# Two decoder blocks on one core: the first modulation, tokens and weight slabs in four groups, and element-wise work moved to GpSimd

## The chip, the core and the metric

The kernel runs on one core of one Trainium2 chip. The metric is the device time of one execution in microseconds (us), the median of the runs shown. TensorE (PE) multiplies matrices, VectorE (DVE) and ScalarE (ACT) do element-wise work, GpSimd (POOL) has been left almost without work so far, and SyncE (SP) issues nearly all DMAs.

## The reference, cut to what matters

512 tokens of width 1024 go through two blocks in float32. The change touches only the beginning of the first:

```
c_act = silu(c)
mod   = c_act @ ada_w + ada_b            # 6 parts of 1024: sh1, sc1, gt1, sh2, sc2, gt2
h     = rms_norm(x, norm_mix_g) * (1 + sc1) + sh1
p     = h @ w_in                          # 896 columns of RWKV, then 512, 768, 256 and 4096 others
y_a   = rwkv7_mixer(p[...])               # y_b: spatial gating, y_c: short convolution, y_d: S5
merged = sum of sigmoid(gate) * y over the four branches
```

The S5 mixer needs tables that depend on its parameters alone: powers of a complex decay (`pw`), times an input matrix (`bb`) or an output matrix (`c4`), for 8 steps each. They are `Q` and `W2`, each a real and an imaginary tile of 128x1024.

## The kernel before, in words

Tokens are kept transposed: 8 tiles of 128 features x 512 tokens. A float32 product is made in three matmuls: each factor is split into an upper half `hi` (ACT, rounded to a type that TensorE takes in one pass) and a lower half `lo` (DVE, the difference), and `mm3` multiplies hi·hi, lo·hi and hi·lo. A weight slab (`wload`) is 128x1024: a DMA into `raw`, `whi` on ACT, `wlo` on DVE. A projection (`proj`) is one slab times the 8 token tiles: 24 matmuls of 128x512.

`_start` opens the program. It broadcasts c over all partitions, makes silu (ACT and DVE), and computes 8 columns of the modulation, each as a DVE dot product of a 128x1024 tile of `ada_w` with `c_row` (`_dot`, shown as CUSTOM_DVE_ANT_0). This is done in two groups of 4 columns; behind each stand 4 token tiles, scaled by `g1` = (1 + sc1) · norm gain and split, and a slab. The RMS norm is not waited for: the seven slabs of RWKV are multiplied with the tokens before their norm, and the rows are scaled afterwards by `rs` (which `means`, `factors` and `spread` make from the sums of squares). `_start_shift` then makes 8 more columns of the modulation and the finished `h`, which every later projection uses. The convolution branch (`cg`, `cy`), the spatial gating (`svp`, `sgz`, `sgm`) and the merges follow.

`_s5_setup` makes the powers with some 120 DVE instructions of a few columns each, `_s5_tables` makes Q and W2 (12 tensor-tensor instructions of 128x1024 by `_cmul`, one negation) and the phases `ph`. TensorE transposes Q (`s5q`) and multiplies it (`s5k`) just before it multiplies `sgm`, which needs `sgz`.

Each engine runs its own queue in order. A scheduler lays the queues out when the program is built; `issue_after(i)` keeps a block's instructions behind instruction i on i's engine. Line numbers are those of the kernel before; in the changed one `_start`'s and later lines stand some 30 to 40 further down.

Of the kernel before, what the change touches and what calls it, by code (L numbers as in the profile page):

```python
# [25 lines left out]
KD = 8  # L26
# [66 lines left out]
class _Core:  # L93
# [230 lines left out]
def _dot(K, raw, src, row, out, scale=1.0, after=None):  # L324

    K.nc.sync.dma_start(raw, src)
    with K.tc.issue_after(after) if after is not None else nullcontext():
        K.nc.vector.tensor_tensor_reduce(raw, raw, row, scale, 0.0, OP.mult, OP.add, out)  # L328


def _ada(K, cols, tag=None, after=None):

    for j in cols:
        if tag is None:
            raw = K.wpool.tile([128, K.WMAX], F32, name="raw", tag="raw", bufs=4)[:, 0:1024]
# [28 lines left out]

def _start(K):

    nc, V = K.nc, K.nc.vector
    K.modv = K.const.tile([128, 48], F32, name="modv")
    K.c_row = K.g("c_row", "cr", shape=(128, D))
    c = K.g("c", "e4", shape=(128, D))  # L370
    nc.sync.dma_start(c, K.dram["c"].partition_broadcast(128))
    nc.scalar.activation(K.c_row, c, AF.Tanh, scale=0.5)
    V.scalar_tensor_tensor(K.c_row, K.c_row, 1.0, c, OP.add, OP.mult)
    g1 = K.const.tile([128, 8], F32, name="g1")
    x, K.h, K.ahead = [], [], []
    for q in range(2):
        ks = slice(4 * q, 4 * q + 4)
        for _ in _ada(K, range(8 + 4 * q, 12 + 4 * q), "e4"):
            pass
        V.scalar_tensor_tensor(g1[:, ks], K.modv[:, 8 + 4 * q:12 + 4 * q], 1.0, K.vec("norm_mix_g", 4 * q, 4),  # L380
                               OP.add, OP.mult)
        if q == 0:
            K.ahead.append(K.wload(K.dram["w_in"][A_ORDER[0]], 8, 128))
        for k in range(4 * q, 4 * q + 4):
            x.append(K.g(f"x{k}", "xr"))
            nc.sync.dma_start(x[k], K.dram["x"][k])
            K.h.append(K.split(x[k], "h", g1[:, k:k + 1]))
        if q == 0:
            K.ahead.append(K.wload(K.dram["w_in"][A_ORDER[1]], 8, 128))
    K.tables()  # L390
    K.split_1 = K.last
    with K.tc.issue_after(K.last):
        v = K.means(K.squares(x, tag="yd"))
    y = K.factors(v, "x")
    K.factored = nc.cur_bb.bb.instructions[-1]
    return x, g1, K.spread(y)


def _start_shift(K, x, g1, rs):
# [363 lines left out]
    return st  # L763


def _rwkv(K, x, g1, rs):

    nc, d = K.nc, K.dram
    tiles = []
    for i, j in enumerate(A_ORDER):  # L770
        ps = K.proj(d["w_in"][j], K.h, w=K.ahead.pop(0) if K.ahead else None)
        p = K.g("rp", "rk")
        nc.scalar.copy(p, ps)
        tiles.append(p)
        if i == SHIFT_AT:
            h = _start_shift(K, x, g1, rs)
    K.h = h
    return tiles


def _rwkv_shift(K, ps, rs):

    nc, d, V = K.nc, K.dram, K.nc.vector
    row = [K.g("sh_row", "yd") for _ in range(2)]
    _row(K, K.modv, row)
    part = K.const.tile([128, 2, 7], F32, name="rk_sp")
    for i, j in enumerate(A_ORDER):
        for q in range(2):
            raw = K.g("w_t", "yd")
            _dot(K, raw, d["w_in_t"][j][:, q * 512:(q + 1) * 512], row[q], part[:, q, j:j + 1],  # L790
                 after=K.sg_normed)
    mu, mu1 = K.vec("rwkv_mu", 0, 7), K.const.tile([128, 7], F32, name="mu1")
    V.tensor_scalar(mu1, mu, -1.0, 1.0, OP.mult, OP.add)
    sv = K.const.tile([128, 2, 7], F32, name="rk_sv")
    V.tensor_tensor(sv[:, 0], part[:, 0], part[:, 1], OP.add)
    V.scalar_tensor_tensor(sv[:, 1], sv[:, 0], -1.0, mu, OP.mult, OP.mult)
    tiles = []
    for p, j in zip(ps, A_ORDER):
# [12 lines left out]
    return la, [tiles[1:4], tiles[4:7]]
# [191 lines left out]
def _s5_tables(K, sp, z):  # L1003
# [8 lines left out]
    w = [128, 8, 8, 16]  # L1012
    pk = lambda z, o: z[:, :, o:o + 8].unsqueeze(3).to_broadcast(w)
    mk = lambda z: z.unsqueeze(2).to_broadcast(w)
    _cmul(V, v4(Q[0]), v4(Q[1]), pk(pr, 0), pk(pi, 0), mk(bb[:, 0]), mk(bb[:, 1]), v4(tq))
    _cmul(V, v4(W2[0]), v4(W2[1]), pk(pr, 1), pk(pi, 1), mk(c4[:, 0]), mk(c4[:, 1]), v4(tq))
    V.tensor_scalar(W2[1], W2[1], -1.0, None, OP.mult)

    cb = K.g("s5_cb", "e", shape=(128, 2, 8, 32))
    nc.gpsimd.memset(cb, 0.0)  # L1020
# [144 lines left out]
def _first_block(K):  # L1165
    nc, d = K.nc, K.dram
    with ExitStack() as mix:
        tags = lambda **n: mix.enter_context(K.tags(**n))
        tags(h=16, y=8, yd=4, rk=8, cr=1)
        tags(space=PSUM, mm=3, sm=5)  # L1170
        tags(side="right", tm=2)
        ada = _ada(K, range(16, 48))
        with K.tags(e=9, e4=8):
            with K.tc.tile_pool(name="s5", bufs=1) as sp:
                x, g1, rs = _start(K)
                tiles = _rwkv(K, x, g1, rs)
# [36 lines left out]
def _feed_forward(K):
# [457 lines left out]
```

## Time and profile before

| what | value |
|---|---|
| median of 3 runs | 2148.33 us (2146.29 to 2150.67) |
| the profiled execution's own time | 2149.2 us |
| its span, first to last instruction | 2147.4 us |
| PE busy | 2094.6 us, 98% of the span |
| DVE busy | 1416.1 us, 66% |
| ACT busy | 934.1 us, 43% |
| POOL busy | 23.5 us, 1% |
| mean granted TensorE clock | 0.992 |

The profiled execution took 1.8 us more than its span, and was 0.9 us above the median. Busy shares are means over stages with different limits; what the change is worth is read in the first 150 us.

### The profile page before, as it was taken

What the parts mean: (1) busy time and instruction counts of PE and PEld (TensorE: products, weight loads), DVE (VectorE), ACT (ScalarE), POOL (GpSimd) and SP (SyncE); (2) the same over time, 40 slices, a digit from 0 to 9 for tenths busy, and PEclk for the clock granted to TensorE, in tenths of its full rate; (3) what the DMA queues carried; (4) which work ended last, traced back from release to release, by engine and by line L of the source; (5) the groups of instructions that cost most, each with busy time, mean ns of one, the idle gap of its engine ahead of it and who ended that gap; (6) DMA issues with size and microseconds to landing.
All of it is one profiled execution on the core that took longest, in us unless ns stands there. A gap on an engine that the chain in (4) does not pass through costs nothing.

```text
span 2147.4 us, 29518 instructions
## 1 busy us (share of the span) xinstructions
PE 2094.6 (98%) x11502; PEld 1692.7 (79%) x11502; DVE 1416.1 (66%) x2655; ACT 934.1 (43%) x1549; POOL 23.5 (1%) x44
## 2 busy tenths in 40 slices
PE   6999999999999999999999999999999999999998
PEld 4877787888888888897778888888887778788887
DVE  7997884755734344558876756747568867575775
ACT  3334432333523232446764423324469944243433
POOL 0010000000000000000000000000000000000000
PEclk9999999999999999999999999999999999999999
DMA  8355441123322232232212222232321122323222
GB/s 329 106 182 180 159 148 50 60 84 133 108 98 89 98 98 89 99 119 89 80 50 98 98 93 94 89 98 81 128 79 40 60 79 86 101 83 105 97 81 67
DMA packets 68091, 220.47 MB, mean 103 GB/s; under 512 B 8068, under 2 KB 11060, under 8 KB 67952
## 3 DMA queue, kind: packets, MB, share of 16 engines
q1 hardware_dynamic: 64704, 210.19, 29.6%
q0 software_dynamic: 2096, 6.30, 1.0%
q8 instruction: 91, 1.49, 0.3%
q10 hardware_dynamic: 1152, 2.10, 0.3%
q14 instruction: 48, 0.39, 0.1%
HBM read 215.25 MB, written 3.30 MB: 102 GB/s over the span
## 4 chain that ended last, share of the span: by engine, by line
PE 85%; DVE 6%; ACT 4%; DMA 2%; issue 1%; DVEq 0%; ACTq 0%; SPq 0%
PE mm L174 62%; PE gp L174 7%; PE vt L174 3%; PE yp L174 2%; DMA raw<-ada_w 2%; PE pT L1336 1%; DVE wlo L153 1%; PE po L1349 1%; PE fin L174 1%; PE s L1316 1%; PE s L1317 1%; ACT whi L152 1%; DVE raw L328 1%; ACT p L1324 1%; PE pmt L643 1%
## 5 line engine op out<-in xcount | busy, mean ns | idle before, releaser
L174 PE MATMUL mm<-hi,whi 128*128 128x512 f32 x2088 | 829.7, 398 | 19.1 <-ACT hi L161 17.8
L174 PE MATMUL mm<-hi,wlo 128*128 128x512 f32 x2088 | 830.5, 398 | 1.1 <-DVE wlo L153 1.1
L174 PE MATMUL mm<-lo,whi 128*128 128x512 f32 x2088 | 829.2, 397 | 1.1 <-DVE lo L165 0.5
L152 ACT ACTIVATE whi<-raw 128x1024 fp32r<-128x1024 f32 (+3 forms) x341 | 350.3, 1030 | 754.9 <-PE mm L174 600.9
L153 DVE TENSOR_TENSOR wlo<-raw,whi 128x1024 fp32r<-128x1024 f32 (+3 forms) x341 | 403.5, 1186 | 180.2 <-ACT whi L152 170.7
L174 PEld LDWEIGHTS mm<-hi,whi 128*128 128x128 f32 x2088 | 395.7, 190 | 110.3 <-ACT hi L161 20.8
L174 PEld LDWEIGHTS mm<-lo,whi 128*128 128x128 f32 x2088 | 394.9, 189 | 91.1 <-DVE lo L165 2.7
L174 PEld LDWEIGHTS mm<-hi,wlo 128*128 128x128 f32 x2088 | 394.7, 189 | 89.9 <-DVE wlo L153 2.0
L1521 DVE TENSOR_TENSOR u<-mm,spr 128x512 f32<-128x512 f32 x88 | 60.6, 688 | 82.5 <-PE mm L174 82.2
L174 PE MATMUL gp<-hi,wlo 128*128 128x512 f32 x256 | 102.7, 401 | 3.3 <-DVE wlo L153 3.3
L174 PE MATMUL gp<-hi,whi 128*128 128x512 f32 x256 | 104.1, 407 | 0.9 <-ACT whi L152 0.9
L174 PE MATMUL gp<-lo,whi 128*128 128x512 f32 x256 | 102.9, 402 | 0.0
L1541 DVE TENSOR_TENSOR x<-x,mm 128x512 f32<-128x512 f32 x48 | 33.0, 687 | 96.1 <-PE mm L174 96.1
L1240 DVE SCALAR_TENSOR_TENSOR x<-mm,modv,x 128x512 f32<-128x512 f32 x32 | 24.0, 751 | 91.0 <-PE mm L174 91.0
L1522 ACT ACTIVATE cv<-u,vecs 128x512 f32<-128x512 f32 x88 | 71.3, 810 | 3.4 <-DVE u L1521 3.2
L1524 DVE SCALAR_TENSOR_TENSOR cv<-u,vecs,cv 128x510 f32<-128x510 f32 x88 | 66.0, 750 | 3.1
L1523 DVE SCALAR_TENSOR_TENSOR cv<-u,vecs,cv 128x511 f32<-128x511 f32 x88 | 65.6, 746 | 2.3 <-ACT cv L1522 2.1
L1532 ACT ACTIVATE cth<-cv 128x512 f32<-128x512 f32 x44 | 27.8, 632 | 86.2 <-DVE cv L1524 86.2
L174 PEld LDWEIGHTS gp<-hi,wlo 128*128 128x128 f32 x256 | 48.4, 189 | 15.6 <-DVE wlo L153 5.1
L1324 ACT ACTIVATE p<-p,at_m 128x128 f32<-128x128 f32 (+1 forms) x96 | 53.4, 557 | 14.7 <-DVE at_m L1323 13.7
L174 PEld LDWEIGHTS gp<-hi,whi 128*128 128x128 f32 x256 | 48.6, 190 | 13.4 <-ACT whi L152 1.8
L174 PEld LDWEIGHTS gp<-lo,whi 128*128 128x128 f32 x256 | 48.6, 190 | 10.6 <-issue 0.4
(532 smaller groups left out, 2612.1 us busy)
## 6 DMA issues: line engine op xcount, KB each, us to landing
raw<-w_up SPq DMA_DIRECT2D x88, 512.0 KB, 3.3
raw<-ffn_w SPq DMA_DIRECT2D x64, 512.0 KB, 3.3
raw<-w_in SPq DMA_DIRECT2D x49, 512.0 KB, 3.4
raw<-ada_w SPq DMA_DIRECT2D x32, 512.0 KB, 3.9
raw<-w_down SPq DMA_DIRECT2D x32, 384.0 KB, 3.1
ada_w<-ada_w SPq DMA_DIRECT2D x16, 512.0 KB, 8.7
raw<-w_out SPq DMA_DIRECT2D x16, 512.0 KB, 3.4
raw<-w_down SPq DMA_DIRECT2D x16, 512.0 KB, 3.3
```

What stands on the lines that cost most here:

```text
L152: nc.scalar.activation(hi[:, :n], raw[:, :n], AF.Copy)
L153: nc.vector.tensor_tensor(lo[:, :n], raw[:, :n], hi[:, :n].bitcast(F32), OP.subtract)
L174: self.nc.tensor.matmul(out, lhsT=a, rhs=b, start=first and n == 0, stop=last and n == total - 1)
L328: K.nc.vector.tensor_tensor_reduce(raw, raw, row, scale, 0.0, OP.mult, OP.add, out)
L1240: V.scalar_tensor_tensor(K.xr[m], ps, K.modv[:, 40 + m:41 + m], K.xr[m], OP.mult, OP.add)
L1324: A.activation(p[:, 0:n], p[:, 0:n], AF.Exp, bias=nm, scale=-1.0, accum_out=l)
L1521: V.tensor_tensor(u, ps, rs, OP.mult)
L1522: A.activation(c, u, AF.Identity, bias=K.vec("conv_b_2", l * 44 + j), scale=tap(2))
L1523: V.scalar_tensor_tensor(c[:, 1:], u[:, 0:S - 1], tap(1), c[:, 1:], OP.mult, OP.add)
L1524: V.scalar_tensor_tensor(c[:, 2:], u[:, 0:S - 2], tap(0), c[:, 2:], OP.mult, OP.add)
L1532: A.activation(th, gt, AF.Tanh, scale=0.5)
L1541: V.tensor_tensor(K.xr[m], K.xr[m], ps, OP.add)
```

## The change

`_start` takes modulation, tokens and slabs in four groups of two instead of two groups of four; c comes in two halves. The first three slabs are loaded there (two before), and their products are issued group by group, two token tiles at a time. Their lower halves, and the additions of the sums of squares, are GpSimd instructions. The squares are queued behind the last `hi` on ACT. Two small DVE instructions that need `vecs` (`mu1`, `gg`) and the S5 setup are queued further back. In `_s5_tables` the 12 products for Q and W2 and the negation are GpSimd instructions.

```diff
 def _start(K):
-    nc.sync.dma_start(c, K.dram["c"].partition_broadcast(128))
-    nc.scalar.activation(K.c_row, c, AF.Tanh, scale=0.5)
-    V.scalar_tensor_tensor(K.c_row, K.c_row, 1.0, c, OP.add, OP.mult)
+    for q in range(2):
+        o = slice(q * 512, (q + 1) * 512)
+        nc.sync.dma_start(c[:, o], K.dram["c"][o].partition_broadcast(128))
+        nc.scalar.activation(K.c_row[:, o], c[:, o], AF.Tanh, scale=0.5)
+        V.scalar_tensor_tensor(K.c_row[:, o], K.c_row[:, o], 1.0, c[:, o], OP.add, OP.mult)
...
-    for q in range(2):
-        ks = slice(4 * q, 4 * q + 4)
-        for _ in _ada(K, range(8 + 4 * q, 12 + 4 * q), "e4"):
-            pass
...
+    def slab():
...
+        nc.sync.dma_start(raw, K.dram["w_in"][A_ORDER[len(w)]])
+        nc.scalar.activation(hi, raw, AF.Copy)
+        G.tensor_tensor(lo, raw, hi.bitcast(F32), OP.subtract)
...
+    def products(i, k0, k1):
+        for k in range(k0, k1):
+            K.mm3(ps[i], [(w[i][0][:, k], w[i][1][:, k])], K.h[k:k + 1], first=k == 0, last=k == KD - 1)
...
+    def squares(k0):
+        for k in (k0, k0 + 1):
+            sq = acc if k == 0 else K.g("rms_q", "yd")
+            with K.tc.issue_after(K.hi_last):
+                nc.scalar.activation(sq, x[k], AF.Square)
+            if k:
+                G.tensor_tensor(acc, acc, sq, OP.add)
...
+    for q in range(4):
+        ks = slice(2 * q, 2 * q + 2)
+        for j in range(8 + 2 * q, 10 + 2 * q):
+            _dot(K, K.g("ada_w", "e4", shape=(128, 1024)), K.dram["ada_w"][j], K.c_row, K.modv[:, j:j + 1], 0.5)
...
         if q == 0:
-            K.ahead.append(K.wload(K.dram["w_in"][A_ORDER[0]], 8, 128))
-        for k in range(4 * q, 4 * q + 4):
+            slab()
+        for k in range(2 * q, 2 * q + 2):
             x.append(K.g(f"x{k}", "xr"))
             nc.sync.dma_start(x[k], K.dram["x"][k])
             K.h.append(K.split(x[k], "h", g1[:, k:k + 1]))
-        if q == 0:
-            K.ahead.append(K.wload(K.dram["w_in"][A_ORDER[1]], 8, 128))
+        if q:
+            squares(2 * q - 2)
+        if q < 2:
+            slab()
+        for i in range(min(q + 2, 3) if q else 2):
+            products(i, done[i], 2 * q + 2)
+            done[i] = 2 * q + 2
...
 def _s5_tables(K, sp, z):
...
-    _cmul(V, v4(Q[0]), v4(Q[1]), pk(pr, 0), pk(pi, 0), mk(bb[:, 0]), mk(bb[:, 1]), v4(tq))
-    _cmul(V, v4(W2[0]), v4(W2[1]), pk(pr, 1), pk(pi, 1), mk(c4[:, 0]), mk(c4[:, 1]), v4(tq))
-    V.tensor_scalar(W2[1], W2[1], -1.0, None, OP.mult)
+    G = nc.gpsimd
+    _cmul(G, v4(Q[0]), v4(Q[1]), pk(pr, 0), pk(pi, 0), mk(bb[:, 0]), mk(bb[:, 1]), v4(tq))
+    _cmul(G, v4(W2[0]), v4(W2[1]), pk(pr, 1), pk(pi, 1), mk(c4[:, 0]), mk(c4[:, 1]), v4(tq))
+    G.tensor_scalar(W2[1], W2[1], -1.0, None, OP.mult)
...
 def _first_block(K):
-                with K.tc.issue_after(K.split_1):
+                with K.tc.issue_after(last):
                     z = _s5_setup(K, sp)
```

On GpSimd's queue, before, a memset of the S5 branch was followed directly by another, and then by the store of `s5_kt`:

```order
L1020 MEMSET s_cb 128x512
L1045 MEMSET s_ti_1745 128x1024
L1041 DMA s_scr<-s_kt 128x256
```

Now, between the same two memsets, stand the lower halves, the sums of squares and the S5 tables (the negation of `s_W_1684` and four more products follow, not shown):

```order
L1060 MEMSET s_cb 128x512
L389 ISA
L389 TENSOR_TENSOR wlo<-raw,whi 128x1024 x2
L405 TENSOR_TENSOR rms_a<-rms_a,rms_q 128x512
L389 TENSOR_TENSOR wlo<-raw,whi 128x1024
L405 TENSOR_TENSOR rms_a<-rms_a,rms_q 128x512 x6
L981 TENSOR_TENSOR s_Q_1681<-s_pw,s_bb 128x1024
L982 TENSOR_TENSOR s_tq<-s_pw,s_bb 128x1024
L984 TENSOR_TENSOR s_Q_1682<-s_pw,s_bb 128x1024
L983 TENSOR_TENSOR s_Q_1681<-s_Q_1681,s_tq 128x1024
L981 TENSOR_TENSOR s_W_1683<-s_pw,s_bc 128x1024
L985 TENSOR_TENSOR s_tq<-s_pw,s_bb 128x1024
```

DVE, in the convolution branch (`cg`, `cy`), had the tables between that branch's instructions and the lower halves of its slabs:

```order
L947 TENSOR_TENSOR s_bb<-s_bb,s_tb 128x128
L870 SCALAR_TENSOR_TENSOR cy<-cg,vecs,cy 128x510
L942 TENSOR_TENSOR s_Q_1674<-s_pw,s_bb 128x1024
L943 TENSOR_TENSOR s_tq<-s_pw,s_bb 128x1024
L863 TENSOR_TENSOR cg<-mm,cg 128x512
L153 TENSOR_TENSOR wlo<-raw,whi 128x1024
L870 SCALAR_TENSOR_TENSOR cy<-cg,vecs,cy 128x511
L944 TENSOR_TENSOR s_Q_1674<-s_Q_1674,s_tq 128x1024
```

In the changed program, behind the last instructions for `bb`, DVE goes on with the convolution branch and the decay of the phases (`s_mag`, `s_sn`), and the products of the tables are gone from its queue:

```order
L983 TENSOR_TENSOR s_bb<-s_bb,s_tb 128x128
L153 TENSOR_TENSOR wlo<-raw,whi 128x1024
L985 TENSOR_TENSOR s_tb<-s_bc,s_qi 128x128
L911 TENSOR_TENSOR cy<-mm,cy 128x512
L986 TENSOR_TENSOR s_bb<-s_bb,s_tb 128x128
L153 TENSOR_TENSOR wlo<-raw,whi 128x1024
L164 TENSOR_TENSOR lo<-cy,hi 128x512
L1096 TENSOR_TENSOR s_mag<-s_mag 128x8
```

Behind the last lower half of the tokens, DVE had the additions of the squares, with the S5 setup between them:

```order
L264 TENSOR_TENSOR rms_a<-rms_a,rms_q 128x512
L961 TENSOR_SCALAR s_lre<-s_par 128x8
L962 COPY s_x<-s_par 128x8
L264 TENSOR_TENSOR rms_a<-rms_a,rms_q 128x512
L202 TENSOR_SCALAR s_x<-s_x 128x8
```

There it now has the two instructions that need `vecs`, and then the norm (`rms_v` waits for TensorE's `rms_p`, which waits for GpSimd's last addition):

```order
L832 TENSOR_SCALAR mu_1636<-vecs 128x7
L1287 TENSOR_TENSOR gg<-vecs 128x8
L276 TENSOR_SCALAR rms_v<-rms_p 128x4
L191 TENSOR_SCALAR rms_y<-rms_v 128x4
L192 TENSOR_SCALAR rms_y<-rms_y 128x4
L153 TENSOR_TENSOR wlo<-raw,whi 128x1024
```

## Rows read from the trace of the kernel before

**Rows 1.** Busy time by engine, from the page: us (share of span) xinstructions.
```profile
PE 2094.6 (98%) x11502; PEld 1692.7 (79%) x11502; DVE 1416.1 (66%) x2655; ACT 934.1 (43%) x1549; POOL 23.5 (1%) x44
```

**Rows 2.** Stages: stretch, length, busy us (xinstructions) by engine, granted clock, DMA, GB/s.
```profile
14.95:29.24 14.29, 11.95 (x34) 8.29 (x35) 12.29 (x21) 7.38 (x12) 0.00 (x0) 1.00 0.99 365
...
44.30:73.00 28.70, 28.70 (x130) 23.47 (x129) 26.84 (x53) 13.10 (x20) 0.96 (x1) 1.00 0.35 118
73.00:100.00 27.00, 27.00 (x119) 21.88 (x118) 26.72 (x99) 8.04 (x10) 0.00 (x0) 1.00 0.29 93
100.00:129.20 29.20, 25.74 (x188) 23.95 (x186) 28.09 (x68) 13.63 (x27) 0.55 (x1) 0.93 0.53 182
140.10:250.00 109.90, 106.33 (x573) 86.81 (x572) 85.19 (x166) 45.07 (x82) 2.51 (x3) 0.98 0.55 177
```

**Rows 3.** Timeline of the start, DVE and PE: start us, length us, engine, line, instruction.
```profile
14.95 0.80 PE L174 MATMUL mm<-hi,whi 128*128 128x512 f32 x1 [14.95 <-ACT hi L161]
...
26.50 2.74 DVE L165 SCALAR_TENSOR_TENSOR lo<-x,g,hi 128x512 fp32r<-128x512 f32 x4 [0.79 <-ACT hi L161]
```

**Rows 4.** Timeline of DVE, around the finished h and the gating.
```profile
37.10 0.16 DVE L275 TENSOR_SCALAR rms_v<-rms_p 128x4 f32<-128x4 f32 x1 [0.52 <-PE rms_p L272]
...
70.92 0.74 DVE L410 SCALAR_TENSOR_TENSOR lo<-x,modv,hi 128x512 fp32r<-128x512 f32 x1
...
128.74 0.74 DVE L917 TENSOR_TENSOR sgz<-sgz,sg_ln 128x256 f32<-128x256 f32 x2
```

**Rows 5.** Timeline of PE: pace of the third slab and the last matmul ahead of `h`.
```profile
37.50 0.63 PE L174 MATMUL mm<-hi,whi 128*128 128x512 f32 x1
37.93 0.63 PE L174 MATMUL mm<-lo,whi 128*128 128x512 f32 x1
...
43.68 0.39 PE L174 MATMUL mm<-lo,whi 128*128 128x512 f32 x1
43.91 0.40 PE L174 MATMUL mm<-hi,wlo 128*128 128x512 f32 x1
```

**Rows 6.** Timeline of PE at the end of the gating's projections.
```profile
117.78 1.95 PE L350 MATMUL row_p<-k_ident,modv 128*128 128x128 f32 x16
119.57 2.18 PE L1031 MATMUL s5q<-k_ident,s_Q 128*128 128x128 f32 x16
...
129.21 1.12 PE L928 MATMUL sgm<-sg_wsT,sgz 128*64 128x128 f32 x8 [3.43 <-DVE sgz L917]
```

**Rows 7.** ACT's first copy of the gating's products, timeline.
```profile
106.57 0.37 ACT L248 COPY gl_x<-svp 128x256 f32<-128x256 f32 x1 [4.04 <-PE svp L174]
```

**Rows 8.** Two of the table products on DVE, timeline.
```profile
88.97 1.22 DVE L942 TENSOR_TENSOR s_Q<-s_pw,s_bb 128x1024 f32<-128x1024 f32 x1
90.10 1.22 DVE L943 TENSOR_TENSOR s_tq<-s_pw,s_bb 128x1024 f32<-128x1024 f32 x1
```

**Rows 9.** POOL's memsets, groups of instructions.
```profile
L1045 POOL MEMSET s_ti<- 128x1024 f32 x2 | 1.9, 964 | 50.6 <-DVE modv L328 50.6
...
L1020 POOL MEMSET s_cb<- 128x512 f32 x1 | 0.6, 563 | 0.0
```

**Rows 10.** POOL's and DVE's timelines around one memset, then around the other.
```profile
132.04 0.97 POOL L1045 MEMSET s_ti<- 128x1024 f32 x1
...
131.71 1.33 DVE L1059 TENSOR_SCALAR s_sn<-s_t 128x8 f32<-128x8 f32 x1
131.78 1.25 DVE L195 SCALAR_TENSOR_TENSOR bn_y<-bn_t,bn_y 128x2 f32<-128x2 f32 x1
131.86 1.19 DVE L1060 TENSOR_SCALAR s_xr<-s_s 128x8 f32<-128x8 f32 x1
...
54.14 0.96 POOL L1045 MEMSET s_ti<- 128x1024 f32 x1 [50.61 <-DVE modv L328]
...
54.69 4.06 DVE L407 SCALAR_TENSOR_TENSOR x<-x,g,spr 128x512 f32<-128x512 f32 x6
```

**Rows 11.** DVE's negation of a table, timeline.
```profile
129.48 0.68 DVE L1017 TENSOR_SCALAR s_W<-s_W 128x1024 f32<-128x1024 f32 x1
```

More of the change, by code (lines that the diff above doesn't have):

```diff
@@ L161, in split @@
         nc.scalar.activation(hi[:, :n], src, AF.Copy, scale=scale)
+        self.hi_last = nc.cur_bb.bb.instructions[-1]
         if isinstance(scale, float) and scale == 1.0:
@@ L365, in _start @@
 def _start(K):
-    nc, V = K.nc, K.nc.vector
+    nc, V, G = K.nc, K.nc.vector, K.nc.gpsimd
     K.modv = K.const.tile([128, 48], F32, name="modv")
@@ L370, in _start @@
     c = K.g("c", "e4", shape=(128, D))
-    nc.sync.dma_start(c, K.dram["c"].partition_broadcast(128))
-    nc.scalar.activation(K.c_row, c, AF.Tanh, scale=0.5)
-    V.scalar_tensor_tensor(K.c_row, K.c_row, 1.0, c, OP.add, OP.mult)
-    g1 = K.const.tile([128, 8], F32, name="g1")
-    x, K.h, K.ahead = [], [], []
-    for q in range(2):
-        ks = slice(4 * q, 4 * q + 4)
-        for _ in _ada(K, range(8 + 4 * q, 12 + 4 * q), "e4"):
-            pass
-        V.scalar_tensor_tensor(g1[:, ks], K.modv[:, 8 + 4 * q:12 + 4 * q], 1.0, K.vec("norm_mix_g", 4 * q, 4),
-                               OP.add, OP.mult)
+    for q in range(2):
[3 more added lines that the diff above has]
+        V.scalar_tensor_tensor(K.c_row[:, o], K.c_row[:, o], 1.0, c[:, o], OP.add, OP.mult)
@@ new lines, in _start @@
+    K.acted = nc.cur_bb.bb.instructions[-1]
+    g1 = K.const.tile([128, 8], F32, name="g1")
+    x, K.h, w, ps = [], [], [], []
+    def slab():
+        raw = K.wpool.tile([128, K.WMAX], F32, name="raw", tag="raw", bufs=4)[:, 0:1024]
+        hi = K.wpool.tile([128, K.WMAX], F32R, name="whi", tag="whi", bufs=3)[:, 0:1024]
+        lo = K.wpool.tile([128, K.WMAX], F32R, name="wlo", tag="wlo", bufs=3)[:, 0:1024]
+        nc.sync.dma_start(raw, K.dram["w_in"][A_ORDER[len(w)]])
+        nc.scalar.activation(hi, raw, AF.Copy)
+        G.tensor_tensor(lo, raw, hi.bitcast(F32), OP.subtract)
+        w.append([t.rearrange("p (k c) -> p k c", k=8) for t in (hi, lo)])
+        ps.append(K.mm())
@@ new lines, in products @@
+    def products(i, k0, k1):
+        for k in range(k0, k1):
+            K.mm3(ps[i], [(w[i][0][:, k], w[i][1][:, k])], K.h[k:k + 1], first=k == 0, last=k == KD - 1)
+    acc = K.g("rms_a", "yd")
+    def squares(k0):
[5 more added lines that the diff above has]
+                G.tensor_tensor(acc, acc, sq, OP.add)
+    done = [0, 0, 0]
@@ L382, in _start @@
+    for q in range(4):
+        ks = slice(2 * q, 2 * q + 2)
+        for j in range(8 + 2 * q, 10 + 2 * q):
+            _dot(K, K.g("ada_w", "e4", shape=(128, 1024)), K.dram["ada_w"][j], K.c_row, K.modv[:, j:j + 1], 0.5)
+        m = K.modv[:, 8 + 2 * q:10 + 2 * q]
+        V.tensor_tensor(m, m, K.vec("ada_b", 8 + 2 * q, 2), OP.add)
+        V.scalar_tensor_tensor(g1[:, ks], m, 1.0, K.vec("norm_mix_g", 2 * q, 2), OP.add, OP.mult)
         if q == 0:
-            K.ahead.append(K.wload(K.dram["w_in"][A_ORDER[0]], 8, 128))
@@ L387, in _start @@
             K.h.append(K.split(x[k], "h", g1[:, k:k + 1]))
-        if q == 0:
-            K.ahead.append(K.wload(K.dram["w_in"][A_ORDER[1]], 8, 128))
+        if q:
[5 more added lines that the diff above has]
+            done[i] = 2 * q + 2
     K.tables()
     K.split_1 = K.last
-    with K.tc.issue_after(K.last):
-        v = K.means(K.squares(x, tag="yd"))
+    squares(6)
+    v = K.means(acc)
     y = K.factors(v, "x")
     K.factored = nc.cur_bb.bb.instructions[-1]
-    return x, g1, K.spread(y)
+    return x, g1, K.spread(y), ps
 def _start_shift(K, x, g1, rs):
@@ L763, in _wkv_consts, with _rwkv @@
     return st
-def _rwkv(K, x, g1, rs):
+def _rwkv(K, x, g1, rs, ahead):
     nc, d = K.nc, K.dram
@@ L770, in _rwkv @@
     for i, j in enumerate(A_ORDER):
-        ps = K.proj(d["w_in"][j], K.h, w=K.ahead.pop(0) if K.ahead else None)
+        ps = ahead[i] if i < len(ahead) else K.proj(d["w_in"][j], K.h)
         p = K.g("rp", "rk")
@@ L792, in _rwkv_shift @@
     mu, mu1 = K.vec("rwkv_mu", 0, 7), K.const.tile([128, 7], F32, name="mu1")
-    V.tensor_scalar(mu1, mu, -1.0, 1.0, OP.mult, OP.add)
+    with K.tc.issue_after(K.split_1):
+        V.tensor_scalar(mu1, mu, -1.0, 1.0, OP.mult, OP.add)
     sv = K.const.tile([128, 2, 7], F32, name="rk_sv")
@@ L1174, in _first_block @@
             with K.tc.tile_pool(name="s5", bufs=1) as sp:
-                x, g1, rs = _start(K)
-                tiles = _rwkv(K, x, g1, rs)
+                x, g1, rs, ahead = _start(K)
+                tiles = _rwkv(K, x, g1, rs, ahead)
                 last = K.last
-                with K.tc.issue_after(K.split_1):
+                with K.tc.issue_after(last):
                     z = _s5_setup(K, sp)
@@ L1245, in _feed_forward @@
     gg = K.const.tile([128, 8], F32, name="gg")
-    V.tensor_tensor(gg, K.vec("final_g", 0, 8), K.vec("norm_mix_2", 0, 8), OP.mult)
+    with K.tc.issue_after(K.split_1):
+        V.tensor_tensor(gg, K.vec("final_g", 0, 8), K.vec("norm_mix_2", 0, 8), OP.mult)
     x = [K.split(K.xr[k], "x", gg[:, k:k + 1]) for k in range(KD)]
```

## Prediction

> **What bounds the kernel now.** The page's first table comes first: PE is busy for 98% of the span, DVE for 66%, POOL for 1% [rows 1]. As a mean this says that only PE's own gaps can be won, 53 us of 2147.4, and that POOL is free. The table of stages says where, and with whom. PE has nothing before 14.95 us, and makes 34 matmuls until 29.24 [rows 2, 3]. From 44.3 to 100 it is busy without a gap, while DVE is busy for 26.8 of 28.7 and 26.7 of 27.0 us: two engines of equal length side by side. From 100 to 129.2 DVE is busy for 28.1 of 29.2 us, and PE loses 3.4: it waits 3.43 us for `sgz` before it can multiply `sgm` [rows 2, 6]. So in the stretch that the change edits DVE paces the program as much as PE does, and the reader should carry one question through all that follows: what does DVE's queue gain or lose? After that PE idles 3.6 us between 140 and 250 [rows 2].
>
> **The start.** [...] Now the first product needs c, two tiles of `ada_w`, one slab and one token tile, 2.25 MB instead of 3.25, and starts some 3 to 4 us sooner. The whole of it is 8 MB, half a MB more than before because a third slab is in it, at 365 GB/s in that stretch [rows 2]: 22 us of transfer. DVE's own part is 8 dots and 8 lower halves, 8 x 1.14 + 8 x 0.68 = 14.6 us: a 128x1024 instruction with two inputs takes 1.22 us and the next starts 1.13 later [rows 8], one of 128x512 takes 4.06 / 6 = 0.68 [rows 10]. Two lower halves of slabs (2.3 us) leave DVE. I put the last lower half of the tokens at 30 us, between 26 (transfers alone) and 34 (if DVE is kept off all the while POOL works, see below). The third slab's last 18 matmuls take 18 x 0.23 = 4.1 us more, and the last four additions of squares on POOL follow one another at about 1.1 us (twice the memset's 0.56 for 128x512 [rows 9], since they read two tiles); both end at about 35, and `rms_v` can start at 35.5. Before it started at 37.10, but with the third slab unfinished [rows 4].
>
> From there DVE's queue has, up to the last lower half of the finished h, 7 lower halves of slabs and 8 dots (15 x 1.14 = 17.1), 21 instructions of 128x512 (13.6) and 24 small ones (1.3, at 0.07 to 0.08 from one to the next [rows 10]): 32.0 us. The setup of S5 no longer stands among them, and POOL has nothing to do then. So h is ready at 67.5; before, at 70.92 + 0.74 = 71.66 [rows 4]. PE gets there earlier (three slabs done at 35, four more at 24 x 0.23 = 5.5) and waits. **Term 1: -4 us**, between 0 and -7.
>
> **The setup of S5 and the gating.** The setup's small instructions now come after h, 99 of them (7.7 us) among 18.2 us of work up to `bb`; the convolution's products, which DVE's queue also waits for, keep this in PE's pace, and `bb` is ready at about 91, when PE is in the convolution. Then come 114 DVE instructions up to the first pair of `sgz`: ten of 128x1024 (11.4), 7 of 512 (3.7), 18 of 256 (5.2), 8 of 128 (1.6), 71 small ones (5.3): 27.2 us, of which 15.8 stand behind the first gelu. That can start when PE's first gating block is copied: 106.57 before [rows 7], 4 us sooner now, and 0.6 for copy and square: 103.2. DVE alone would get there at 91 + 11.4 = 102.4. So without any hindrance `sgz` is ready at 103.2 + 15.8 = 119. PE comes to `sgm` at about 120: 129.2 less 4, less its wait of 3.4, less the 1.8 of `row_p` (117.78 to 119.57 [rows 6]), which now fills a gap before h. That is -9 us, and PE would not fall to the slow pace behind the wait, 2 us more.
>
> **What POOL's work costs DVE.** No row of this trace has a POOL instruction that reads tiles, so its length is bounded: the memset of 128x1024, which only writes, takes 0.96 us [rows 9]; two reads and a write in turn at that pace would be 2.9. I take two passes, 1.9. The tables are 12 such and a negation of one pass: 23.8 us (12.5 to 36).
>
> DVE and POOL are not independent. At 132.04 POOL runs its memset for 0.97 us, to 133.01. Three DVE instructions of 8 columns around it, issued at 131.71, 131.78 and 131.86, take 1.33, 1.25 and 1.19 us and all end at about 133.04 [rows 10]; one of 4 columns takes 0.16 otherwise [rows 4]. DVE was held for the whole POOL instruction. At 54.14 the same memset runs beside scalar-tensor-tensors of 128x512, and those keep their 0.68 us each [rows 10]. What differs? [...] The two-input ones write one tile, and read two. By this reading a POOL instruction that reads two tiles will hold nearly every DVE instruction here, for its whole length; that it holds none is the other end, since the two-input ones passed the memset unharmed. I take the hold: the one collision that the trace shows was complete, and nothing of DVE's 27.2 us but a few copies from PSUM and statistics is of another kind.
>
> [...]
>
> DVE is in step with PE in that stretch (0.8 us to spare), so of 23.8 us some 23 go to `sgz`: 119 + 23 = 142 instead of 129.2. PE waits there, or before, for the lower halves of its slabs, which stand in the same queue. **Term 2: +13 us** in place of the -9, term 1 included. The same hold at the start is in my 30 us above.
>
> **Given back later.** The phases and the decay, about 60 small instructions, are done before `sgz` now and behind it before; the gaps of 3.6 us between 140 and 250 can shrink by about 2 us. **Term 3: -2.** S5's own use of Q comes 8 tables after `bb`, 8 x 1.9 and as many DVE instructions between: before 115, ahead of PE. The rest of the program, where PE is alone the bound, only moves.
>
> **Sum.** 13 - 2 = +11 on a span of 2147.4: 2158.4. The profiled execution took 1.8 us more than its span and 0.9 more than the median: 2159.
>
> **The rivals.**
> (a) POOL's instructions pass DVE's by as the memset at 54.14 did. Then `sgz` and `sgm` come at 120, -9, and 2 us of slow pace go: 2148 - 11 = 2137. For it: that row; against it: the held three. Chance 0.32.
> (b) DVE is held for less than half, because POOL waits for DVE as often as DVE for POOL, or because its instructions are as short as the memset. With 12.5 us of hold `sgz` comes at 119 + 12 = 131, +2 - 2: no change, 2148. The point from which it decides: 10 us lost by DVE. Chance 0.14, of which 0.09 within 0.2%.
> (c) POOL needs 2.9 us or more for each: 36 us of hold, +25 - 2, and Q's second half comes at 91 + 8 x 3.6 = 120, when PE asks for it: 2171. Chance 0.10.
> (d) The forecast, hold at 1.9 us: chance 0.44, its own range 2151 to 2168.
>
> **How the numbers follow.** About 0.2% of the time, 4 us, is what a measurement of this kernel can tell from no change. Faster: (a) and a little of (b), 0.34. Same: 0.09. Slower: (c), (d) and the rest of (b), 0.57. The range takes in (a) and reaches nearly to (c): 2133 to 2170.
>
> **What the profile of the changed kernel would show.** Right: between 90 and 130 us DVE instructions of a few columns that take 1 to 2 us and end with a POOL instruction; POOL at about 1.9 us for 1024 columns; PE waiting for `sgz` or for a `wlo` for more than 10 us before `sgm`, which starts after 138; h ready at about 67.5. Wrong: two-input DVE instructions of unchanged length beside POOL's, and `sgm` at 120. If POOL's instructions are stretched instead, the hold falls on the engine that has time, and (b) or (a) follows.

## The result, and the profile after

The changed kernel takes 2174.5 us (median of 4 runs, 2172.88 to 2176.02) against 2149.5 for the kernel before on the same chip: a ratio of 1.0119 (95%: 1.0103 to 1.0135). It is slower, as forecast, but by 25 us where 11 were forecast, outside the range of 2133 to 2170. Its profiled execution has a span of 2171.1 us, 23.7 more than before.

Four moments say where the 23.7 us arise:

| moment | before | after | forecast |
|---|---|---|---|
| `rms_v` starts | 37.10 | 44.84 | 35.5 |
| last lower half of h ends | 71.66 | 80.71 | 67.5 |
| first `sgm` starts | 129.2 | 156.0 | 142 |
| span | 2147.4 | 2171.1 | 2158.4 |

The second and the third in the trace after (DVE's timeline, then PE's):

```profile
79.96 0.75 DVE L448 SCALAR_TENSOR_TENSOR lo<-x,modv,hi 128x512 fp32r<-128x512 f32 x1
...
156.04 1.12 PE L967 MATMUL sgm<-sg_wsT,sgz 128*64 128x128 f32 x8 [2.33 <-issue]
```

From h to `sgm` the forecast had 74.5 us and the kernel took 75.3. So the miss, 13.2 us, was there before h was ready.

First the page's busy row by engine, which answers [rows 1]:

```profile
PE 2095.0 (96%) x11502; PEld 1693.0 (78%) x11502; DVE 1429.7 (66%) x2637; ACT 934.6 (43%) x1550; POOL 72.3 (3%) x67
```

DVE has 18 instructions less and is busy for 13.6 us more: some of its instructions became longer. Next the table of stages, as [rows 2]:

```profile
81.00:102.84 21.84, 21.84 (x96) 17.70 (x95) 20.81 (x116) 7.60 (x9) 0.00 (x0) 1.00 0.23 74
102.84:134.50 31.66, 10.34 (x58) 9.32 (x57) 31.60 (x35) 2.33 (x3) 31.02 (x14) 0.67 0.11 36
134.50:160.00 25.50, 23.17 (x147) 21.12 (x147) 24.73 (x98) 10.72 (x23) 1.74 (x5) 0.83 0.51 168
```

Read the second row across: POOL busy for 31.0 of 31.7 us, DVE "busy" for 31.6 with 35 instructions, where the stage before had 116 in a shorter time, and PE for 10.3. The busy time of a held instruction includes the hold. DVE's and POOL's timelines in that stretch show it:

```profile
107.11 2.43 DVE L164 TENSOR_TENSOR lo<-cy,hi 128x512 fp32r<-128x512 f32 x1
109.46 1.89 DVE L1096 TENSOR_TENSOR s_mag<-s_mag 128x8 f32<-128x8 f32 x1
111.28 0.15 DVE L1097 TENSOR_TENSOR s_t<-s_sn,s_xr 128x8 f32<-128x8 f32 x1
111.35 2.31 DVE L1098 TENSOR_TENSOR s_s<-s_sn 128x8 f32<-128x8 f32 x1
113.58 0.15 DVE L1096 TENSOR_TENSOR s_mag<-s_mag 128x8 f32<-128x8 f32 x1
113.69 1.86 DVE L1099 TENSOR_SCALAR s_sn<-s_t 128x8 f32<-128x8 f32 x1
...
130.77 0.68 DVE L911 TENSOR_TENSOR cy<-mm,cy 128x512 f32<-128x512 f32 x1
```
```profile
108.96 2.38 POOL L984 TENSOR_TENSOR s_Q<-s_pw,s_bb 128x1024 f32<-128x1024 f32 x1
111.29 2.34 POOL L983 TENSOR_TENSOR s_Q<-s_Q,s_tq 128x1024 f32<-128x1024 f32 x1
113.60 1.93 POOL L981 TENSOR_TENSOR s_W<-s_pw,s_bc 128x1024 f32<-128x1024 f32 x1
115.49 1.92 POOL L985 TENSOR_TENSOR s_tq<-s_pw,s_bb 128x1024 f32<-128x1024 f32 x1
```

The two lists interlock. `s_mag` of 8 columns, 0.15 us by itself, takes 1.89 and ends at 111.35 with the POOL instruction that began at 108.96; `s_s` takes 2.31 and ends with the next. For each POOL instruction one DVE instruction is held to its end, and one or two get through while POOL starts its next. POOL is slowed too: five of its eight multiplications take 1.92 to 1.94 us, the other three 2.38 to 3.06. (The four sums and differences of two whole tiles take 2.34 to 2.59; in no run is one below 2.33.) Between 104.6 and 130.8 us DVE gets 26 instructions done, 22 of them of 8 columns (the decay of the phases), and behind them stands the second `cy`. PE's waits, longest first, and PE's timeline around the longest:

```profile
PE svp L175 <- DVE cy L911: 21.3, 1, 21.3
PE mm L175 <- ACT hi L161: 14.7, 2, 13.4
PE mm L175 <- DVE lo L166: 2.8, 2, 1.6
PE sgm L967 <- issue: 2.3, 1, 2.3
```
```profile
109.79 0.28 PE L175 MATMUL svp<-wlo,hi 128*128 128x256 f32 x1
109.90 0.28 PE L175 MATMUL svp<-whi,lo 128*128 128x256 f32 x1
131.51 0.58 PE L175 MATMUL svp<-whi,hi 128*128 128x256 f32 x1 [21.32 <-DVE cy L911]
131.88 0.42 PE L175 MATMUL svp<-wlo,hi 128*128 128x256 f32 x1
132.10 0.42 PE L175 MATMUL svp<-whi,lo 128*128 128x256 f32 x1
```

PE stops for 21.3 us in the gating's first product. It comes back with 0.22 us from one matmul to the next instead of 0.12, at a granted clock of 0.50 from 131.5 to 135.0, and the granted clock of the next stage is 0.83 on the mean. This is the slow pace of the forecast: before, behind the wait for `sgz`, the granted clock was 0.50 from 129.2 to 133.0, and matmuls of 128x512 came 0.43 us apart, where 0.23 is usual.

At the start the same thing happens with the slabs' lower halves and the sums of squares (DVE's timeline, then POOL's):

```profile
13.38 5.16 DVE L166 SCALAR_TENSOR_TENSOR lo<-x,g,hi 128x512 fp32r<-128x512 f32 x2 [1.34 <-ACT hi L161]
...
24.48 2.30 DVE L329 CUSTOM_DVE_ANT_0 ada_w<-ada_w,c_row 128x1024 f32<-128x1024 f32 x1
...
26.83 2.17 DVE L413 TENSOR_TENSOR modv<-modv,vecs 128x2 f32<-128x2 f32 x1
...
37.05 1.41 DVE L166 SCALAR_TENSOR_TENSOR lo<-x,g,hi 128x512 fp32r<-128x512 f32 x2 [0.79 <-ACT hi L161]
...
44.84 0.16 DVE L276 TENSOR_SCALAR rms_v<-rms_p 128x4 f32<-128x4 f32 x1 [5.12 <-PE rms_p L273]
```
```profile
12.82 2.41 POOL L389 TENSOR_TENSOR wlo<-raw,whi 128x1024 fp32r<-128x1024 f32 x1 [9.26 <-ACT whi L388]
15.46 2.54 POOL L389 TENSOR_TENSOR wlo<-raw,whi 128x1024 fp32r<-128x1024 f32 x1 [0.23 <-ACT whi L388]
...
25.66 3.32 POOL L389 TENSOR_TENSOR wlo<-raw,whi 128x1024 fp32r<-128x1024 f32 x1
...
38.29 5.40 POOL L405 TENSOR_TENSOR rms_a<-rms_a,rms_q 128x512 f32<-128x512 f32 x4 [3.52 <-ACT rms_q L403]
```

A pair of lower halves, 1.41 us by itself, takes 5.16 beside two `wlo`. An addition of 2 columns, 0.16 by itself, takes 2.17. From the first dot at 8.56 to the last lower half at 38.46 are 29.9 us, of which 9.0 are such holds (3.75 in the first pair, 2.0 in the addition, 1.1 in each of three dots).

### The profile page after: what moved, and what is told of

Same layout as the page of the kernel before. It is cut to its first block, busy times and chain, and to the rows that moved or that the text cites. A ratio compares the mean times of both kernels' runs of the same rounds, so it can differ in the third digit from the quotient of the medians.

```text
span 2171.1 us, 29540 instructions
## 1 busy us (share of the span) xinstructions
PE 2095.0 (96%) x11502; PEld 1693.0 (78%) x11502; DVE 1429.7 (66%) x2637; ACT 934.6 (43%) x1550; POOL 72.3 (3%) x67
## 4 chain that ended last, share of the span: by engine, by line
PE 86%; DVE 6%; ACT 4%; DMA 2%; issue 1%; POOL 0%; SPq 0%; DVEq 0%; ACTq 0%; POOLq 0%
PE mm L175 63%; PE gp L175 7%; PE vt L175 3%; PE yp L175 2%; PE pT L1377 1%; PE po L1390 1%; PE s L1357 1%; PE fin L175 1%; DVE wlo L153 1%; DMA raw<-ada_w 1%; PE s L1358 1%; ACT p L1365 1%; ACT whi L152 1%; PE svp L175 1%; PE pmt L681 0%
## 5 line engine op out<-in xcount | busy, mean ns | idle before, releaser
L1365 ACT ACTIVATE p<-p,at_m 128x128 f32<-128x128 f32 (+1 forms) x96 | 53.4, 557 | 14.8 <-DVE at_m L1364 14.0
L175 PEld LDWEIGHTS gp<-hi,whi 128*128 128x128 f32 x256 | 48.2, 188 | 13.2 <-ACT whi L152 1.8
L1377 PE MATMUL pT<-k_ident,p 128*128 128x128 f32 x304 | 53.9, 280 | 3.0 <-ACT p L1374 2.5
```

The costliest lines, as they stand in the source:

```text
L175: self.nc.tensor.matmul(out, lhsT=a, rhs=b, start=first and n == 0, stop=last and n == total - 1)
L1365: A.activation(p[:, 0:n], p[:, 0:n], AF.Exp, bias=nm, scale=-1.0, accum_out=l)
L1377: T.transpose(pp[:, b * 128:(b + 1) * 128], p[:, b * 128:(b + 1) * 128], K.ident)
```

## Experiments

The theory is that GpSimd instructions that read tiles hold DVE's (theory 1). Its rival is that the new order costs the time, with the setup of S5 behind h, and that GpSimd is only a witness (theory 2). The first four kernels take the change apart. Measured values stand in the table below.

**e1**, in `_s5_tables`:
```diff
-    G = nc.gpsimd
+    G = nc.vector
```


> The changed kernel with only the S5 tables back on DVE (13 instructions); slabs' lower halves and sums of squares stay on GpSimd. Theory 1 (GpSimd instructions that read tiles hold DVE's): the 18 us between h ready and the gating's product come back, except what 14 us of tables on DVE cost; the start stays 9 us late: about 2158 us (2153 to 2164), h ready still at about 80 us, first sgm about 140. Theory 2 (the new order, with the setup of S5 behind h, is what costs; GpSimd is only a witness): DVE gets 14 us more to do in the stretch in which it is late already: 2174 to 2186.

**e2**, in `_start`:
```diff
-        G.tensor_tensor(lo, raw, hi.bitcast(F32), OP.subtract)
+        V.tensor_tensor(lo, raw, hi.bitcast(F32), OP.subtract)
-                G.tensor_tensor(acc, acc, sq, OP.add)
+                V.tensor_tensor(acc, acc, sq, OP.add)
```


> The changed kernel with the three lower halves and the seven additions of squares back on DVE; the tables stay on GpSimd. Theory 1: the start's hold goes, h is ready at 68 to 73 us instead of 80.7 and the time falls by 8 to 12, to about 2164; the tables' hold stays (first sgm about 146). Theory 2: the start is late because it is cut into four groups with the loads in another order; h stays at about 80 or later, time 2172 to 2180.

**e3**: both edits.

> The changed kernel with nothing moved to GpSimd: four groups and the new places of the setup alone. Theory 1: both holds gone; h ready at 68 to 73, first sgm at 122 to 132, time 2143 to 2153. Theory 2: the order costs the 25 us, so 2170 or more.

**e4**: the kernel before, with the change's four lines in `_s5_tables` alone.

> The kernel before with only the tables moved to GpSimd. Theory 1: DVE loses 14 us of tables and gains about 25 us of hold where it paces the program: first sgm at 135 to 145 instead of 129.2, time 2155 to 2164. Theory 2: DVE is simply relieved of 14 us: first sgm 3 us earlier, 2140 to 2147.

| kernel | on GpSimd | `rms_v` | h | `sgm` | span | median | ratio to before (95%) |
|---|---|---|---|---|---|---|---|
| after | start, tables | 44.84 | 80.7 | 156.0 | 2171.1 | 2174.5 | 1.0119 (1.0103 to 1.0135) |
| e1 | start | 45.91 | 80.6 | 136.8 | 2152.6 | 2154.9 | 1.0020 (1.0011 to 1.0030) |
| e2 | tables | 38.99 | 72.5 | 147.6 | 2167.5 | 2169.1 | 1.0090 (1.0075 to 1.0105) |
| e3 | nothing | 38.88 | 74.0 | 129.2 | 2146.4 | 2147.1 | 0.9987 (0.9974 to 1.0000) |
| e4 | tables, rest as before | 37.80 | 71.2 | 146.6 | 2170.2 | 2171.4 | 1.0096 (1.0080 to 1.0112) |

Theory 2 falls: the new order without GpSimd (e3) costs nothing, and the tables on GpSimd cost 21.8 us with the rest of the kernel as before (e4). The parts add up: from e3 to e2 the tables cost 22.0 us and from e3 to e1 the start 7.8, together 29.8; from e3 to the changed kernel it is 27.4. e1 and e3 came out as theory 1 expected, but for e3's h at 74.0 instead of 73 at the latest. e2 and e4 were missed in size: putting the start back wins 5.4 us, not 8 to 12, and e4's 2171.4 lies above the 2164 expected at most.

In e4 5.4 us are lost behind `sgm` (17.4 there, 22.8 at the end). Its first `sgm` is not quite the same moment as in the others, since its queues were laid out otherwise: 26 of the 32 `s5k`, which all stand ahead of `sgm` in the kernel before, stand behind it. At the 0.11 us from one to the next these are some 3 of the 5.4 us, an estimate. PE also waits 4.7 us for one `wlo` there, which DVE starts at 250.91, behind 10 us that are nearly all S5's products and scans. Why these stand there was not followed.

**e6 and e7: what must GpSimd's instruction do to hold DVE's?** In place of the eleven tensor-tensors behind the first product, and of the negation, stand 23 memsets (e6), or eleven copies and the negation (e7).

```diff
-    _cmul(G, v4(Q[0]), ...)
-    _cmul(G, v4(W2[0]), ...)
-    G.tensor_scalar(W2[1], W2[1], -1.0, None, OP.mult)
+    G.tensor_tensor(v4(Q[0]), pk(pr, 0), mk(bb[:, 0]), OP.mult)
+    for t_ in (tq, Q[0], Q[1], tq, Q[1], W2[0], tq, W2[0], W2[1], tq, W2[1]):
+        for _ in range(2):
+            G.memset(t_, 0.0)            # e7: G.tensor_copy(o_, i_), once for each
+    G.memset(W2[1], 0.0)
```


> The changed kernel with the S5 tables left out but for their first product: in place of the other twelve GpSimd instructions stand 23 memsets of the same tiles, which only write, so S5's output is not the reference's. GpSimd is kept busy for some 24 us in the same place. Theory 1 (what holds DVE is that GpSimd reads): the two-input instructions of DVE go by unharmed, only copies and tensor-scalars of a few columns are held; cy and sgz come as early as PE allows, first sgm at 128 to 136, time 2146 to 2153. Theory 2 (any work of GpSimd's on SBUF holds DVE): PE waits some 20 us for cy as before, first sgm after 150, time 2168 or more.

> The changed kernel with the tables left out but for their first product: eleven GpSimd copies of one tile of 128x1024 to another and the negation stand in their place, so S5's output is not the reference's. Theory 1 (one read of GpSimd's is enough to hold a two-input DVE instruction): DVE instructions end with GpSimd's again, one for one; at 1 to 2 us for a copy 12 to 24 us are lost, first sgm at 138 to 152, time 2155 to 2170. Theory 2 (only two inputs against two inputs collide): first sgm at 128 to 136, time 2146 to 2153.

e6 takes 2171.4 us (1.0112; 1.0099 to 1.0126), with `sgm` at 153.4: the time that theory 2 named. But its trace does not show what theory 2 says. DVE's timeline, then one of POOL's memsets:

```profile
105.82 1.21 DVE L153 TENSOR_TENSOR wlo<-raw,whi 128x1024 fp32r<-128x1024 f32 x1
106.95 0.68 DVE L164 TENSOR_TENSOR lo<-cy,hi 128x512 fp32r<-128x512 f32 x1
107.55 0.15 DVE L1098 TENSOR_TENSOR s_mag<-s_mag 128x8 f32<-128x8 f32 x1
...
107.89 16.65 DVE L1101 TENSOR_SCALAR s_sn<-s_t 128x8 f32<-128x8 f32 x1
107.97 16.58 DVE L1102 TENSOR_SCALAR s_xr<-s_s 128x8 f32<-128x8 f32 x1
108.05 16.51 DVE L1098 TENSOR_TENSOR s_mag<-s_mag 128x8 f32<-128x8 f32 x1
...
107.48 0.96 POOL L1058 MEMSET s_tq<- 128x1024 f32 x1
```

While memsets of 0.96 us follow one another on POOL, the two-input instructions keep their length. The first tensor-scalar, of 8 columns, is held for 16.65 us, through 18 memsets, and everything stands behind it; the two next in the queue show nearly the same length. So writes alone do not hold the two-input ones, and they hold a tensor-scalar without giving way between one memset and the next. The expectation, `sgm` at 128 to 136, left no room for that: in [rows 10] the hold is that of one memset.

e7 takes 2162.0 us (1.0066; 1.0050 to 1.0082), `sgm` at 143.9, as theory 1 expected. Its timeline of DVE, beside copies of 1.04 to 1.08 us:

```profile
109.55 0.98 DVE L1101 TENSOR_SCALAR s_sn<-s_t 128x8 f32<-128x8 f32 x1
...
110.63 0.99 DVE L1099 TENSOR_TENSOR s_t<-s_sn,s_xr 128x8 f32<-128x8 f32 x1
...
119.41 1.51 DVE L164 TENSOR_TENSOR lo<-cy,hi 128x512 fp32r<-128x512 f32 x1
```

One tile read by GpSimd is enough to hold a two-input DVE instruction: `s_t` of 8 columns takes 0.99 us instead of 0.15, `lo` of 512 takes 1.51 instead of 0.68.

**e13 and e14: does it matter what DVE has to do there?** The block for the decay and the phases goes under `with K.tc.issue_after(K.sg_normed):`, in the changed kernel (e13) and in e6 (e14).

> The changed kernel with the decay and the phases of S5 (DVE instructions of a few columns) issued behind the gating's normalisation; all GpSimd work as in the changed kernel. Theory 1 (each GpSimd instruction of the tables costs DVE its length, whatever DVE has there): PE waits less for cy and more for sgz; first sgm at 150 to 156, time 2167 to 2174. Theory 2 (the loss comes from short instructions held in front of cy, and longer ones share the time better, or the holds fall where DVE would wait for PE anyway): cy comes 10 to 20 us earlier, first sgm at 138 to 146, time 2157 to 2165.

> The kernel with 23 write-only memsets in place of the tables (left out but for their first product), with the decay and the phases behind the gating. In the run without this edit one tensor-scalar of 8 columns was held for 16.65 us. If only copies and tensor-scalars are held by writes, nothing of that kind stands ahead of cy now: PE does not wait for cy, first sgm at 128 to 138 (a tensor-scalar of the gelu may be held by the last memsets), time 2147 to 2156. If memsets hold other instructions too: 2165 or more.

e13: 1.0075 (1.0057 to 1.0094), `sgm` at 146.8; its median of 2168.0 stands beside 2152.4 of the kernel before in those runs. That is between the theories, nearer the second at `sgm`: 9 us are won there with the same work on POOL. PE no longer waits for `cy`; DVE's big instructions are held now. DVE's timeline, and PE's two waits ahead of `sgm`:

```profile
112.58 2.87 DVE L164 TENSOR_TENSOR lo<-cy,hi 128x512 fp32r<-128x512 f32 x1
115.37 2.96 DVE L153 TENSOR_TENSOR wlo<-raw,whi 128x1024 fp32r<-128x1024 f32 x1
...
PE sgm L967 <- ACT s_kt L1079: 9.9, 1, 9.9
PE mm L175 <- ACT gl_s L250: 4.9, 1, 4.9
```

The holds beside the thirteen GpSimd instructions sum to 21.0 us over DVE's own lengths, against 21.9 in the changed kernel, but PE waits 14.8 us there instead of 23.6. So the same hold costs PE more or less by what stands behind it in DVE's queue. Some of the 9 us is lost later: PE waits 4.5 us for `s_xb`, which needs the phases.

e14: 1.0042 (1.0026 to 1.0057), `sgm` at 140.1. PE does not wait for `cy`, but the first tensor-scalar that comes now, one of the gelu's, is held until the memsets are nearly done:

```profile
112.64 1.22 DVE L153 TENSOR_TENSOR wlo<-raw,whi 128x1024 fp32r<-128x1024 f32 x1
113.90 11.22 DVE L251 TENSOR_SCALAR gl_s<-gl_s 128x256 f32<-128x256 f32 x1
```

I had allowed for the last memsets there, not for 11 us of them, and so `sgm` and the time lie above what I expected.

**e8 and e9: which part of the start?** e3 with one of e2's two lines back on GpSimd.

> Four groups with only the seven additions of squares on GpSimd; halves and tables on DVE. With everything on DVE it was 2147.1, with halves and additions on GpSimd 2154.9. Theory A (each us of GpSimd's at the start costs DVE alike): additions are 10.6 of 18.9 us of GpSimd's, so 4.4 of the 7.8: 2151.5, and rms_v at 42. Theory B (only the last four additions count, 5.4 us in front of rms_v): 6 to 8 us, 2153 to 2155, rms_v at 44 to 45.

> Four groups with only the three lower halves of slabs on GpSimd; additions and tables on DVE. Theory A: 8.3 of 18.9 us of GpSimd's, so 3.4 of the 7.8: 2150.5, and rms_v at 41. Theory B: nothing, 2146.5 to 2148, rms_v at 39.

e8: 1.0041 (1.0028 to 1.0053), `rms_v` at 42.41; e9: 1.0008 (0.9999 to 1.0017), 41.70. At `rms_v` theory A holds: 3.5 and 2.8 us over e3, 6.3 together; with both it is 6.0 in the changed kernel and 7.0 in e1. In the whole time they do not add. By the ratios e9 costs 4.5 us over e3, near theory A's 3.4, but e8 costs 11.6, above both theories, where e1 with both costs 7.1 (the intervals of e8 and e1 overlap a little). In e8 PE waits 5.3 us for `sgz` and 1.8 for `sh_row`; why was not settled.

**e5, e10, e11, e12: a better version?** e5 is e3 with `issue_after(K.split_1)` for the setup again. e10 is e3 with the second `_cmul` and the negation under `issue_after(K.sg_normed)`. e11 has both, and e12 is e10 with that half on GpSimd.

> Four groups, nothing moved to GpSimd, and the setup of S5 back at its old place, before h. If DVE's queue between h and the gating is what PE waits for in the run without GpSimd work (6.8 us before the first sgm), it is 6 to 7 us shorter now: first sgm at 123 to 127, time 2141 to 2145. If the setup only moves the same wait in front of h, h comes 3 to 6 us later and the time stays at 2146 to 2149.

> Four groups, nothing on GpSimd, and the second half of the S5 tables (seven DVE instructions, 7.5 us) is issued behind the gating's normalisation. Two of them stood ahead of the first pair of sgz and five ahead of the second. First sgm 2 to 3 us earlier, the second pair 7; time 2142 to 2146. If PE does not wait for sgz but for something else there, no change: 2147.

> Both edits, the old place of the setup and the late second half. If each takes its own share of PE's wait before sgm: 2139 to 2144, the best of all; if they share one wait, the better of the two.

> The late second half of the tables on GpSimd instead of DVE, so that its 14 to 18 us lie behind the first sgm. Theory 1 (each GpSimd instruction that reads costs DVE one hold wherever DVE is busy): DVE, busy for 19 of 20 us there, loses 14 to 18 us and is spared 7.5; PE waits for lower halves behind the gating instead of before it: 2148 to 2154. Theory 2 (the hold matters only ahead of the gating): 2142 to 2146 as with the late half on DVE, or better.

| kernel | h | `sgm` | span | median | ratio (95%) |
|---|---|---|---|---|---|
| e5 | 70.4 | 129.3 | 2145.5 | 2144.6 | 0.9982 (0.9972 to 0.9992) |
| e10 | 73.9 | 127.8 | 2149.3 | 2150.8 | 1.0009 (1.0000 to 1.0017) |
| e11 | 68.8 | 125.1 | 2146.0 | 2148.5 | 1.0001 (0.9992 to 1.0009) |
| e12 | 74.2 | 138.9 | 2154.5 | 2156.6 | 1.0039 (1.0026 to 1.0053) |

e5 is the fastest of all and beats both kernels, by 0.18% of the one before; from e3 it can't be told apart. Its time lies in the first of the expected ranges, but its `sgm` did not move (129.3), so the reason given there is not shown. Its h comes 3.6 us ahead of e3's, but there the six `rp` of 128x512 (4.1 us) stand ahead of h's last lower half and here behind it. e10 and e11, expected at 2142 to 2146 and 2139 to 2144, are misses: they bring `sgm` 1.4 and 4.1 us forward and lose it again behind it (in e11 PE waits 4.1 us for `s_xb`, a later step of S5). e12, above both its theories, misses its purpose: POOL runs ahead of the place in DVE's order, makes two of the products between 95 and 101 us and the rest between 115.7 and 129.5, ahead of `sgm`. It shows that half of the tables on GpSimd costs 11 us over e3 by the ratios, half of what all cost.

## Why the direction was right and the size wrong

**Start (term 1, -4 us): wrong, it was +9.** This is the step that failed, and it is the whole miss: 13.2 us at h, where the sum is 12.7 short at the end. It has three pieces.
- The last lower half of the tokens, put at 30, came at 38.46. I had taken the transfers' 26 as the bound and added 4 us for the hold. The hold took 9.0. What is left, 29.5, is DVE's queue and not the transfers: 4.6 of the 29.9 us from the first dot on are idle (29.90 less DVE's busy 25.29), and only 0.6 of these is a wait for a transfer. 3.7 are hand-overs: each of the four groups waits for ACT's `hi` between its dots and its lower halves, 1.34 us in the first and 0.79 in the others. My sum had DVE's instructions and no hand-over. In e3, with nothing on GpSimd and the slabs' lower halves back on DVE, the last pair ends at 34.31 (first row below). The first product starts at 13.40, 1.6 us sooner than before and not 3 to 4. The 0.23 us a matmul of my sum is the pace at which the third slab ended before, 43.68 to 43.91 [rows 5].
- From there to `rms_v` 6.4 us instead of 5.5. The additions of squares take 1.35 us where nothing holds them (5.40 for four, DVE nearly idle), not 1.1.
- DVE's queue from `rms_v` to h took 35.9 instead of 32.0 (second row below): DVE is busy for 33.0 and waits for 2.9, among it 1.2 for PE's products and 1.1 for ACT. The 33.0 is what my own rates give: 21 x 0.68 is 14.3, not 13.6, and 24 at 0.07 to 0.08 are 1.7 to 1.9, not 1.3. The same stretch takes 34.6 before and 35.1 in e3. A sum of a queue's instructions is its lower bound, and I used it as the time.

```profile
32.90 1.41 DVE L166 SCALAR_TENSOR_TENSOR lo<-x,g,hi 128x512 fp32r<-128x512 f32 x2 [0.79 <-ACT hi L161]
...
44.84:80.71 35.87, 34.61 (x150) 27.91 (x150) 32.97 (x60) 12.89 (x19) 0.00 (x0) 0.90 0.43 136
```

Even without GpSimd the four groups bring nothing at h: it is at 74.0 in e3, 2.3 later than before, and at 72.5 in e2, whose instructions up to there are the same (the granted clock from `rms_v` to h is 0.95 in e3 and 1.00 in e2). The 70.4 of e5 and the 68.8 of e11 are not comparable, since six `rp` stand behind h there. So no run shows the 4 us.

**Tables (term 2): the size right, in part by luck.** Hold of 23 us forecast; the held instructions between 104.6 and 130.8 sum to 21.9 over their own lengths, and h to `sgm` took 75.3 instead of 74.5 (75.1 in e2). GpSimd's price of 1.9 us was right for the eight multiplications (1.92 to 1.94 at the least) and low for the four sums (2.33 at the least) and the negation (put at 1.0, 2.78 at the least in any run; on DVE it took 0.68 [rows 11]). The thirteen took 30.8 us from the first start to the last end instead of 23.8. Part of that is DVE holding GpSimd: the first product began at 102.84 while a `wlo` of DVE ran to 103.90, and ended at 105.90, 2.00 after it. So the hold was 21.9 of 30.8, not the whole length. That PE waits more than 10 us ahead of `sgm` was right, but not for `sgz` or a slab's lower half: it waits 21.3 us for `cy` and 2.3 at `sgm`. And e13 takes 9 us from `sgm` with the same POOL work and nearly the same hold, so the agreement rests on what stood in DVE's queue, which I had not used: short instructions, ten of which pay 1.7 to 2.2 us each ahead of `cy`. The 119 us without any hindrance, from which the sum starts, is not shown: no run has the tables off DVE and nothing held.

**Reason for the hold: right.** I took from [rows 10] that a read by GpSimd holds a two-input DVE instruction and a write doesn't; no run had shown such a read then. e7 and e6 show both halves: the `lo` of 128x512, 0.68 us by itself, takes 2.43 beside products in the changed kernel, 1.51 beside copies in e7, and 0.68 beside memsets in e6. Why a read holds it and a write does not, no run shows. One reading on the way was wrong: of the three held instructions in [rows 10], taken there as of one kind and of 8 columns, the middle one, `bn_y`, has two inputs and 2 columns. It stood in the queue behind a held tensor-scalar, and e6 shows that such a one shows the same length (16.51 us for a tensor-tensor behind the 16.65).

**Given back (term 3, -2): near in size, the reason not shown.** 26.8 us at `sgm`, 23.7 at the end: -3.1. In the 119 us from the first `sgm` on PE idles 2.7 us instead of 3.6 before, so only 0.9 came from the gaps that I named. e2, with the phases in the same place, gives nothing back (18.4 us at `sgm`, 20.1 at the end), and runs of the kernel before differ by 7 us among themselves.

**The rivals.** (a), POOL passes DVE by, is ruled out by every held row; (b) by the 21.9 us. (c) came nearest in time, 2171, for another reason than it gave: GpSimd's products did not need 2.9 us by themselves (1.92 and 2.33 at the least), and Q was in time (its last product ends at 121.9, PE asks at 148.3).

## What to carry to other kernels

An idle GpSimd is not free help for a DVE that paces the program. Here DVE was held 12 times beside 13 GpSimd instructions that read tiles, each time for 1.1 to 2.2 us beyond its own length, and the tables cost 22 us more on GpSimd than on DVE. Count for a move not the work that leaves DVE but the length of what GpSimd then does beside it, and look which instructions of DVE's will stand there, and what waits behind them. A short one pays as much as a long one: `s_mag` of 8 columns lost 1.74 us in the changed kernel, a `wlo` of 128x1024 1.74 in e13. When the time of a stage is summed from one engine's instructions, add the hand-overs to the other engines, which come once for each group.

## What was not expected of the hardware

Back-to-back memsets on GpSimd held one DVE tensor-scalar of 8 columns for 16.65 us, through 18 instructions, and one of 256 columns for 11.22; both came through only when two or three memsets were left. GpSimd's reading instructions let DVE in after each: beside the thirteen of the changed kernel 26 of DVE's came through, and no hold there was longer than 2.2 us. The hold goes both ways: a GpSimd multiplication of 128x1024 takes 1.92 us at the least and 3.06 where a `wlo` of DVE was running when it began.
